# Longer runs of half-array fp32 products, and forget-gate and sparse queries and keys computed transposed, in a two-block transformer kernel

## The chip, the cores and the metric

The kernel runs on one core of one Trainium2 chip. The metric is device time in microseconds (us) of one execution: the median of several runs. The engines named below are PE (TensorE, matrix products, with its weight loads listed apart as PEld), DVE (VectorE), ACT (ScalarE), POOL (GpSimd) and SP (SyncE, which here issues nearly all transfers).

## The reference

Two transformer blocks over 256 tokens of width 1024, all in fp32. Only what the change touches is shown. In the first block one projection of the normalised input gives four attention branches: A (sparse: compressed, selected and windowed keys; 4 heads of 64), B (dilated; 3 groups of 2 heads of 64), C (forgetting; 4 heads of 64) and D (latent; 4 heads of 96).

```python
def nsa_mixer(q, kv_a, ...):                                   # branch A
    k_cmp, v_cmp, k_slc, v_slc, k_win, v_win = split(kv_a, 6)
    kc = gelu((blocks(k_cmp) + cmp_pos) @ phi_k_w1) @ phi_k_w2 # 15 blocks of 32*64 numbers, hidden width 128
    vc = gelu((blocks(v_cmp) + cmp_pos) @ phi_v_w1) @ phi_v_w2
    # softmax(q kc), softmax(q k_slc + bias), softmax(q k_win + bias), each times its values, mixed by gates
def forgetting_mixer(q, k, v, f_logits, f_bias):               # branch C
    cum = cumsum(log_sigmoid(f_logits + f_bias))
    logits = q k / 8 + cum[query] - cum[key]                   # causal softmax, then times v
```

In the second block a retention of 8 heads of 64 computes (q k^T * decay) v without a softmax, and a differential attention of 4 heads forms two causal softmaxes of 64-wide queries and keys each.

## The kernel before

All tensors stay on the chip; the weights stream in from HBM, mostly as panels of 128 x 1024 numbers (512 KB). A panel is loaded by SP into one of 3 `raw` buffers, and `W` (L479) splits it into two parts: `hi`, a copy rounded by ACT, and `lo`, the remainder, by DVE (8 buffers each). The large products (`lin` L597, `mm3` L492) are three single-pass products: hi by hi, hi by lo, lo by hi. `lin` has the input as the stationary operand and gives tokens on partitions ("natural"): 48 products of 512 columns for 512 outputs. `linT` (L624) has 128 weight columns stationary and gives the result transposed, outputs on partitions: 8 products of 512 columns and 8 of 256 for 128 outputs.

The attention products are plain fp32, and each of them shows as two instructions in the trace. Those of heads 64 wide use half of the PE array: in `scores` (L645) the two heads of a pair stand on partitions 0 to 63 and 64 to 127 and are issued in turn (form 64*128 in the trace), and in `values` (L675) the two heads' results go to partitions 0 to 63 and 64 to 127 (form 128*64). `plan.glue()` keeps the four products of such a call together in PE's order. `attend` (L684) is scores, softmax and values of one pair. In branch C the queries and keys are natural (`evac1` L891), get two more columns that carry the cumulated gate, so 66 in all, and 16 PE transposes turn them (L975). Branch A's queries and keys are natural too (`evac2` L962, `evac3` L984) and are turned by 12 transposes (L995). The compressed keys of branch A come from L1065 to L1121: their weights `w1` go through `W` as four panels, the 15 blocks of keys and of values, in hi and lo parts, are a stationary operand of 60 columns, and 16 products with `hi` and 16 with `lo` accumulate. Retention (L1453) has four pairs of heads, each with one run of scores and 6 products of 64 columns with the full array; the differential attention (L1482) has one run of scores for each head.

Every instruction is first recorded. A planner (`Plan`, L17) then simulates the engines, with a cost for each instruction (`_Op`, L347) and the buffers as slots (8 PSUM banks among them), repeats this 120 times with changed priorities, and issues all in the order of the shortest simulated run. So the order on each engine and on SP's queue is fixed by the planner's costs, and each change of a cost may change all of the order.

Of the kernel before, what the change touches and what calls it, by code (L numbers as in the profile page):

```python
# [20 lines left out]
class Plan:  # L21
# [137 lines left out]
    @contextmanager  # L159
    def glue(self):  # L160

        self.gluing = True
        yield
        self.gluing, self.glued = False, None

    def trial(self, prio):
# [29 lines left out]
        while done < len(ops):  # L196
# [15 lines left out]
            for e, hp in heaps.items():  # L212
# [3 lines left out]
                while hp:  # L216
                    pr, n = heapq.heappop(hp)
                    if n in ran:
                        o = None
                        continue  # L220
                    o = ops[n]
                    ok = True
                    for nm in o.own:
                        if nm in place:
                            continue
                        c = self.cls[nm]
                        need = 1 if order[c][ptr[c]] == nm else 1 + (99 if o.dma else self.reserve.get(c, 99))
# [122 lines left out]
class _Op:  # L350
    def __init__(self, plan, n, eng, go, name, outs, ins, k):
# [8 lines left out]
        elif eng == "PE":  # L360
            n_ = size if name == "matmul" else 128
            if name == "transpose":
                self.cost = 108.0
            elif ins[0].dtype == F32R:
# [53 lines left out]
def emit(ctx, tc, nc, T, out, dbg):  # L418
# [226 lines left out]
    def scores(qk, bias, mn, at):  # L645

        ps = [psS([128, 384]) for _ in qk]
        ss = [sb([128, 384], "k2", name="s") for _ in qk]  # L650
        plan.hold = list(ss)
        with plan.glue():
            for tt in (1, 0):
                for p, (q, k) in zip(ps, qk):
                    PE.matmul(p[:, COLS[tt]], q[:, tt * 128:tt * 128 + 128], k[:, :128 * (tt + 1)], start=True, stop=True)
        for tt in (1, 0):
            for u, (p, s) in enumerate(zip(ps, ss)):
                c = at(tt, u)
                V.tensor_tensor_reduce(s[:, COLS[tt]], p[:, COLS[tt]], bias[u][tt], 1.0, 3e38, op0=OP.add, op1=OP.min,
                                       accum_out=mn[:, c:c + 1])  # L660
        return ss
# [13 lines left out]
    def values(po, pts, vs, first, last):  # L675

        blocks = ((0, slice(0, 256), slice(0, 256)), (1, slice(128, 256), slice(256, 384)))
        with plan.glue():
            for n, (j, c, w) in enumerate(blocks if first else blocks[::-1]):
                for u in range(2):  # L680
                    PE.matmul(po[64 * u:64 * u + 64, c], vs[u][j], pts[u][:, w], start=first and n == 0,
                              stop=last and n == 1, skip_group_check=first and last)

    def attend(po, qk, bias, vs, gain=None, first=True, last=True):  # L684

        mn, den, rec = small(4), small(4), small(4)
        ss = scores(qk, bias, mn, lambda tt, u: 2 * tt + u)
        for tt in (1, 0):
            for u in range(2):
                c = slice(2 * tt + u, 2 * tt + u + 1)  # L690
                expo(ss[u], tt, mn[:, c], den[:, c])
        V.reciprocal(rec, den)
        if gain is not None:
            for tt in range(2):
                V.tensor_mul(rec[:, 2 * tt:2 * tt + 2], rec[:, 2 * tt:2 * tt + 2], gain(tt))
        for u in range(2):
            for tt in (1, 0):
                AN.scale(ss[u][:, COLS[tt]], ss[u][:, COLS[tt]], rec[:, 2 * tt + u:2 * tt + u + 1])
        pts = [transP(s) for s in ss]
        values(po, pts, vs, first, last)  # L700
# [17 lines left out]
def mats1(E):  # L718
# [170 lines left out]
    cq, ck, cv = {}, {}, {}  # L889

    def evac1(_, tt, acc):  # L891
        a = acc.rearrange("p (b h d) -> p b h d", b=2, h=4)
        q = sb([128, 4, 66], "k2", name="cq")
        k = sb([128, 4, 66], "k2", name="ck")
        S.mul(q[:, :, :64], a[:, 0], rq8[tt])
        V.tensor_scalar(k[:, :, :64], a[:, 1], rx[tt], None, op0=OP.mult)
        cum = cps[:, tt, :]
        V.tensor_scalar(q[:, :, 64], cum, -1.0, None, op0=OP.mult)
        V.memset(q[:, :, 65], 1.0)
        V.memset(k[:, :, 64], 1.0)  # L900
        V.tensor_copy(k[:, :, 65], cum)
        cq[tt], ck[tt] = q, k

    lin(h, [(two(T["wi1"]), 512)], evac1)
# [43 lines left out]
    def plain(q, k, v, kd, key):  # L948

        oT = heads(key, 2)  # L950
        for p in range(2):
            hs = (2 * p, 2 * p + 1)
            po = psS([128, 256])
            attend(po, [(q[:kd, h], k[:kd, h]) for h in hs], [(cm(0), cm(1))] * 2,
                   [[v[j][:, h, :] for j in range(2)] for h in hs])
            outT(oT, p, po)
# [3 lines left out]
    aqd = {}  # L960

    def evac2(_, tt, acc):  # L962
        v = sb([128, 4, 64], "k1", name="cv")
        V.tensor_scalar(v.rearrange("p h d -> p (h d)"), acc[:, :256], rx[tt], None, op0=OP.mult)
        cv[tt] = v
        q = sb([128, 256], "k1", name="aq")
        S.mul(q, acc[:, 256:], rq8[tt])
        aqd[tt] = q

    lin(h, [(two(T["wi2"]), 512)], evac2)  # L970

    cqT = sb([128, 4, 256], "k4", name="cqT")
    ckT = sb([128, 4, 256], "k4", name="ckT")
    for tt in range(2):
        for src, dst, e in ((cq[tt], cqT, 0), (ck[tt], ckT, 1)):  # L975
            tp = psS([128, 4, 128])
            for i in range(4):
                PE.transpose(tp[:66, i, :], src[:, i, :], ident)
            AN.copy(dst[:66, :, tt * 128:tt * 128 + 128], tp[:66])
    plain(cqT, ckT, cv, 66, "c")  # L980

    akn, av = {}, {}

    def evac3(_, tt, acc):  # L984
        k = sb([128, 4, 2, 64], "k2", name="ak")
        S.mul(k, acc[:, :256].rearrange("p (c d) -> p c d", c=4)[:, :, None, :].to_broadcast([128, 4, 2, 64]), rx[tt])
        v = sb([128, 128], "k1", name="av")
        V.tensor_scalar(v, acc[:, 256:384], rx[tt], None, op0=OP.mult)
        akn[tt], av[tt] = k, v

    lin(h, [(two(T["wi3"]), 384)], evac3)

    aqT = sb([128, 2, 256], "k4", name="aqT")
    akT = sb([128, 4, 256], "k4", name="akT")
    for tt in range(2):  # L995
        tp = psS([128, 2, 128])
        for i in range(2):
            PE.transpose(tp[:, i, :], aqd[tt][:, i * 128:(i + 1) * 128], ident)
        AN.copy(aqT[:, :, tt * 128:tt * 128 + 128], tp)
        tp = psS([128, 4, 128])  # L1000
        for i in range(4):
            PE.transpose(tp[:, i, :], akn[tt][:, i].rearrange("p a d -> p (a d)"), ident)
        AN.copy(akT[:, :, tt * 128:tt * 128 + 128], tp)
# [5 lines left out]
    def evac4(_, tt, acc):  # L1009
        bv[tt] = bvs[:, tt]  # L1010
        S.mul(bv[tt].rearrange("p a b -> p (a b)"), acc, rx[tt])
# [4 lines left out]
    for c in range(6):  # L1016
        acc = linT(h, T["wi5"][c], psA)
        t = sb([128, 256], "k1", name="bqk")
        if c < 3:
            S.mul(t, acc[:, 0], -0.125)  # L1020
            V.scalar_tensor_tensor(t, acc[:, 1], -0.125, t, op0=OP.mult, op1=OP.add)
        else:
            S.copy(t, acc[:, 0])
            V.tensor_add(t, acc[:, 1], t)
        V.tensor_mul((bq if c < 3 else bk)[:, c % 3], t, rT)
# [36 lines left out]

    gate(0, "d")

    posT = sb([128, 16], "sm", name="posT")  # L1065
    G.dma_start(posT, T["posT"])
    w2 = sb([128, 2, 64], "k1", name="w2")
    G.dma_start(w2, T["w2"])
    blk = sb([128, 16, 60], "k8", F32R, name="blk")
    for kv in range(2):  # L1070
        t = sb([128, 16, 15], "k1", name="blkf")
        for par in range(2):
            base = akT[par * 64:(par + 1) * 64, kv, par:par + 1]
            src = bass.AP(tensor=base.tensor, offset=base.offset, ap=[list(base.ap[0]), [2, 16], [16, 15]])
            V.tensor_add(t[par * 64:(par + 1) * 64], src,
                         posT[par * 64:(par + 1) * 64, :, None].to_broadcast([64, 16, 15]))
        hh = blk[:, :, 15 * kv:15 * kv + 15]
        S.copy(hh, t)
        V.tensor_sub(blk[:, :, 30 + 15 * kv:45 + 15 * kv], t, f(hh))
    hp = psS([60, 256])  # L1080
    for c in range(4):
        hi, lo = W(T["w1"][c], 1024)
        for i in range(4):
            k = 4 * c + i
            w = slice(i * 256, (i + 1) * 256)
            if k == 15:
                PE.matmul(hp[:30], blk[:, k, :30], lo[:, w], start=False, stop=False)
            PE.matmul(hp, blk[:, k, :], hi[:, w], start=k == 0, stop=k == 15)
            if k < 15:
# [670 lines left out]
```

## Time and profile before

| what | value |
|---|---|
| time, median of 3 runs | 871.64 us (871.44 to 871.86) |
| time of the profiled execution | 872.01 us |
| span of the profiled execution | 870.2 us, mean granted clock 0.997 |
| PE busy | 858.7 us, 99% |
| DVE busy | 663.0 us, 76% |
| ACT busy | 479.5 us, 55% |
| POOL busy | 45.3 us, 5% |
| chain that ended last | PE 89%, DVE 5%, issue 2% |

The span runs from the first instruction to the last, and the profiled execution's own time lies 1.8 us above it. Busy time is the union of an engine's instructions; matrix products overlap at their ends, so the time that one of them costs PE is read from start to start in the timeline, not from its length.

### The profile page before, as it was taken

The numbers are of one execution on the slowest core, as the hardware profiler recorded it, in microseconds if no ns is written. First come the engines' busy times: TensorE is split into PE (matmuls) and PEld (weight loads), VectorE is DVE, ScalarE is ACT, GpSimd is POOL, SyncE is SP. The second block draws the span as 40 slices with busy tenths as digits, with TensorE's granted clock in tenths as the row PEclk, the third lists the DMA queues.
The fourth block names the chain that finished last, engine by engine and source line by source line (L and its number), as shares of the span: only waits on it lengthen the run. The fifth ranks groups of instructions, "written<-read, shape, count | busy, mean of one in ns | idle before, by whom it ended". The sixth has DMA issues, their size and how long they took to land.

```text
span 870.2 us, 12251 instructions
## 1 busy us (share of the span) xinstructions
PE 858.7 (99%) x4453; PEld 719.8 (83%) x4453; DVE 663.0 (76%) x1201; ACT 479.5 (55%) x810; POOL 45.3 (5%) x58
## 2 busy tenths in 40 slices
PE   8999999999999999999999999999999999999998
PEld 7789877778887888888878887888888888888886
DVE  6986766775778999898988677968775687776663
ACT  5775564764555766655654357645644545544440
POOL 2100000000001000000010111201100000000000
PEclk9999999999999999999999999999999999999999
DMA  7657745466447666666536564454643566666641
GB/s 225 207 191 217 218 148 164 160 198 213 144 148 241 195 212 211 204 195 192 193 122 198 167 194 149 143 169 145 208 131 97 187 200 216 215 182 185 198 141 49
DMA packets 45200, 156.07 MB, mean 179 GB/s; under 512 B 5142, under 2 KB 6984, under 8 KB 45012
## 3 DMA queue, kind: packets, MB, share of 16 engines
q1 hardware_dynamic: 44228, 153.09, 56.1%
q0 software_dynamic: 896, 2.19, 0.8%
q8 instruction: 35, 0.57, 0.3%
q14 instruction: 25, 0.20, 0.1%
q10 hardware_dynamic: 16, 0.00, 0.0%
HBM read 154.21 MB, written 1.06 MB: 178 GB/s over the span
## 4 chain that ended last, share of the span: by engine, by line
PE 89%; DVE 5%; issue 2%; ACT 1%; DMA 1%; POOL 1%; DVEq 0%; POOLq 0%; ACTq 0%
PE bank L102 89%; DVE k L102 2%; DVE lo L102 1%; DVE x L102 1%; POOL sm L102 1%; DMA raw<-in_fdn 1%; DMA raw<-in_fupn 1%; ACT x L102 0%; DVE sm L102 0%; ACT junk L102 0%; ACT k L102 0%; ACT hi L102 0%; ACT k L112 0%; DVEq L1756 0%; ACT sm L102 0%
## 5 line engine op out<-in xcount | busy, mean ns | idle before, releaser
L102 PE MATMUL bank<-hi,x 128*128 128x512 f32 (+3 forms) x1556 | 494.3, 392 | 2.2 <-DVE x L102 1.4
L102 DVE TENSOR_TENSOR lo<-raw,hi 128x1024 fp32r<-128x1024 f32 (+3 forms) x280 | 334.7, 1203 | 79.5 <-ACT hi L102 77.9
L102 ACT CAST hi<-raw 128x1024 fp32r<-128x1024 f32 (+3 forms) x280 | 288.7, 1036 | 140.2 <-PE bank L102 57.9
L102 PEld LDWEIGHTS bank<-hi,x 128*128 128x128 f32 (+1 forms) x1556 | 288.5, 188 | 57.6 <-ACT hi L102 2.5
L102 PE MATMUL bank<-lo,x 128*128 128x512 f32 (+3 forms) x786 | 305.7, 391 | 2.7 <-DVE lo L102 2.2
L102 PEld LDWEIGHTS bank<-lo,x 128*128 128x128 f32 (+1 forms) x786 | 146.6, 187 | 33.0 <-DVE lo L102 4.5
L102 PE MATMUL bank<-x,hi 128*128 128x512 f32 x656 | 167.9, 392 | 0.0
L102 PEld LDWEIGHTS bank<-x,hi 128*128 128x128 f32 x656 | 119.2, 189 | 21.3
L102 PEld LDWEIGHTS bank<-x,lo 128*128 128x128 f32 x656 | 89.7, 190 | 6.5
L102 PE MATMUL bank<-x,lo 128*128 128x256 f32 x656 | 91.8, 282 | 0.0
L112 ACT COPY k<-bank 128x256 f32<-128x256 f32 (+3 forms) x78 | 31.1, 409 | 56.8 <-PE bank L102 52.3
L102 POOL TENSOR_TENSOR sm<-sm,nhalf 128x1 f32<-128x1 f32 (+3 forms) x36 | 35.8, 997 | 492.8 <-DVE sm L102 492.8
L102 PE MATMUL bank<-ident,k 128*128 128x128 f32 (+3 forms) x347 | 53.3, 275 | 1.0 <-DVE k L102 0.7
L102 PEld LDWEIGHTS bank<-ident,k 128*128 128x128 f32 (+3 forms) x347 | 41.5, 138 | 13.8 <-DVE k L102 4.7
L102 DVE TENSOR_TENSOR x<-bank,x 128x512 fp32r<-128x512 f32 (+4 forms) x62 | 36.2, 606 | 20.4 <-PE bank L102 19.4
L102 PE MATMUL bank<-k,k 64*128 64x256 f32 (+12 forms) x364 | 49.9, 327 | 0.7 <-ACT k L112 0.6
L102 PEld LDWEIGHTS bank<-k,k 64*128 64x128 f32 (+4 forms) x364 | 38.7, 176 | 11.5 <-issue 4.9
L102 DVE COPY k<-bank 128x256 f32<-128x256 f32 (+7 forms) x60 | 28.1, 473 | 22.3 <-PE bank L102 22.0
L102 DVE TENSOR_TENSOR k<-k,bank 128x256 f32<-128x256 f32 (+1 forms) x78 | 32.5, 418 | 8.2 <-ACT k L112 7.5
L102 ACT ACTIVATE k<-bank,sm 128x256 f32<-128x256 f32 (+1 forms) x38 | 20.0, 554 | 28.4 <-PE bank L102 17.4
L102 DVE SCALAR_TENSOR_TENSOR k<-k,k,k 128x255 f32<-128x255 f32 x72 | 34.3, 479 | 1.5 <-ACT k L102 0.7
L102 ACT ACTIVATE k<-k,sm 128x128 f32<-128x128 f32 (+1 forms) x60 | 26.6, 446 | 7.5 <-DVE sm L102 7.4
(121 smaller groups left out, 439.4 us busy)
## 6 DMA issues: line engine op xcount, KB each, us to landing
raw<-in_wi SPq DMA_DIRECT2D x42, 512.0 KB, 4.4
raw<-in_up SPq DMA_DIRECT2D x40, 512.0 KB, 4.1
raw<-in_fup SPq DMA_DIRECT2D x36, 512.0 KB, 4.3
raw<-in_wg SPq DMA_DIRECT2D x32, 512.0 KB, 4.3
raw<-in_fdn SPq DMA_DIRECT2D x22, 512.0 KB, 4.5
raw<-in_dn SPq DMA_DIRECT2D x22, 512.0 KB, 4.6
raw<-in_xkv SPq DMA_DIRECT2D x16, 512.0 KB, 4.3
raw<-in_wo SPq DMA_DIRECT2D x8, 512.0 KB, 4.4
```

The source lines that it names most:

```text
L102: op = _Op(self, n, eng, lambda: getattr(target, name)(*map(self.place, a), **{x: self.place(y) for x, y in k.items()}), name, outs, ins, k)
L112: alt = _Op(self, n, e2, lambda: getattr(t2, n2)(*map(self.place, a2), **k2), n2, outs, ins, k2)
```

## The change

Five things change together.

1. `scores`, `values` and `attend` take a list of jobs, and the products of all jobs stand in one glued group. Branches C and D and the differential attention put two pairs (or two heads) in a group, branch A its two kinds of keys, branch B two pairs and one pair for scores and three pairs for values.
2. Retention's scores are grouped by two pairs. Its values use `values` too, which leaves them transposed, so each pair is copied and turned back by two transposes: 8 more transposes and 4 more copies.
3. Queries and keys of C and A come from `linT` (`turned`). C's gate term is no longer in two more columns: a tile of bias, written to DRAM as 8 rows of 128 and read back on all partitions (512 KB), is combined with the mask by 8 DVE instructions. A's two key pairs are also copied to the other half of the partitions by 4 transfers. All of this is issued by SP. The 28 transposes of C and A and the copies after them go.
4. The compressed keys use fp32 weights as they are: no `W`, and 32 products of 128 columns in which 15 stationary columns go in turn to partitions 0, 32, 64 and 96 of the result, in two glued groups.
5. The planner charges half-array and 15-column products less and each glued group 300 ns more, and lets a group take several buffers of a kind at once.

```diff
-    def glue(self):
+    def glue(self, extra=300.0):
         self.gluing = True
         yield
+        self.glued.cost += extra
         self.gluing, self.glued = False, None
...
+            elif plan.gluing and m == 15:
+                self.cost = n_ / 2.4 + 2.0
+            elif plan.gluing and (m == 64 or p == 64):
+                self.cost = n_ * 2 / 2.4 + 2.0
...
-    def scores(qk, bias, mn, at):
+    def scores(jobs):
...
         with plan.glue():
+            for j, pj in zip(jobs, ps):
+                for tt in (1, 0):
+                    for p, (q, k) in zip(pj, j[0]):
+                        PE.matmul(p[:, COLS[tt]], q[:, tt * 128:tt * 128 + 128], k[:, :128 * (tt + 1)], start=True, stop=True)
...
+    def turned(c, ap, dst, q):
+        acc = linT(h, ap, psA)
+        t = sb([128, 256], "k1", name="trn")
+        if q:
+            AN.scale(t, acc[:, 0], -0.125)
+            V.scalar_tensor_tensor(t, acc[:, 1], -0.125, t, op0=OP.mult, op1=OP.add)
+        else:
+            AN.copy(t, acc[:, 0])
+            V.tensor_add(t, acc[:, 1], t)
+        V.tensor_mul(dst, t, rT)
+    cum = sb([128, 8], "sm", name="cum")
...
+    nc.sync.dma_start(scr2, crow)
...
+    nc.sync.dma_start(fox1, bass.AP(tensor=scr2.tensor, offset=scr2.offset, ap=[[0, 128], [1, 1024]]))
...
+    for hh in range(4):
+        V.scalar_tensor_tensor(fox0[:, hh], fox1[:, hh, :128], cum[:, 2 * hh:2 * hh + 1], cm(0), op0=OP.subtract, op1=OP.add)
+        V.scalar_tensor_tensor(fox1[:, hh], fox1[:, hh], cum[:, 2 * hh + 1:2 * hh + 2], cm(1), op0=OP.subtract, op1=OP.add)
+    for c in range(4):
+        turned(c, T["wi1"][c], cqk[:, c], c < 2)
...
-    lin(h, [(two(T["wi3"]), 384)], evac3)
...
+    for c in range(4):
+        turned(c, T["wi3"][c], aqk[:, c], c < 2)
+        if c >= 2:
+            for u in range(2):
+                nc.sync.dma_start(aks[64 * (1 - u):64 * (2 - u), c - 2], aqk[64 * u:64 * u + 64, c])
...
-    for c in range(4):
-        hi, lo = W(T["w1"][c], 1024)
...
+    hp = psS([128, 128])
+    for cc in ((0, 1), (2, 3)):
+        ws = [sb([128, 1024], "g4", name="w1") for c in cc]
...
+        with plan.glue():
+            for c, w in zip(cc, ws):
+                for i in range(4):
+                    for kv in range(2):
+                        r = 32 * (2 * (i % 2) + kv)
+                        PE.matmul(hp[r:r + 15], blk[:, kv, 4 * c + i], w[:, i * 256 + kv * 128:i * 256 + kv * 128 + 128],
+                                  start=c == 0 and i < 2, stop=c == 3 and i > 1)
...
-            PE.matmul(po[0][:, h, :], d[:, :128], rv[0][:, h, :], start=True, stop=True)
-            PE.matmul(po[1][:, h, :], d[:, 128:256], rv[0][:, h, :], start=True, stop=False)
-            PE.matmul(po[1][:, h, :], d[:, 256:], rv[1][:, h, :], start=False, stop=True)
...
+        pT = [psS([128, 256]) for _ in pp]
+        values([(pT[i], ds[i], [[rv[j][:, 2 * p + u, :] for j in range(2)] for u in range(2)], True, True)
+                for i, p in enumerate(pp)])
+        for i, p in enumerate(pp):
+            oT = sb([128, 256], "k1", name="rT")
+            AN.copy(oT, pT[i])
+            for tt in range(2):
+                PE.transpose(po[tt][:, 2 * p:2 * p + 2, :].rearrange("p h d -> p (h d)"), oT[:, tt * 128:tt * 128 + 128], ident)
```

## Rows read from the trace of the kernel before

**Rows 1.** The page: busy us of each engine, its share, instructions

```profile
PE 858.7 (99%) x4453; PEld 719.8 (83%) x4453; DVE 663.0 (76%) x1201; ACT 479.5 (55%) x810; POOL 45.3 (5%) x58
```

**Rows 2.** Waits of PE: total us, times, longest us

```profile
PE bank L102 <- DVE lo L102: 2.2, 3, 1.0
```

**Rows 3.** Timeline of PE, one score run: start us, us, names, form, count

```profile
117.19 0.39 PE L102 MATMUL bank<-hi,x 128*128 128x512 f32 x1
117.51 0.92 PE L102 MATMUL bank<-k,k 64*128 64x256 f32 x8
118.36 0.50 PE L102 MATMUL bank<-hi,x 128*128 128x512 f32 x1
118.70 0.40 PE L102 MATMUL bank<-lo,x 128*128 128x512 f32 x1
```

**Rows 4.** Timeline of PE, a run of three score groups

```profile
534.21 2.23 PE L102 MATMUL bank<-k,k 64*128 64x256 f32 x24
536.38 0.50 PE L102 MATMUL bank<-lo,x 128*128 128x512 f32 x1
```

**Rows 5.** Timeline of PE, a run of two value groups

```profile
147.83 1.52 PE L102 MATMUL bank<-k,k 128*64 128x256 f32 x16
149.28 0.50 PE L102 MATMUL bank<-hi,x 128*128 128x512 f32 x1
```

**Rows 6.** Timeline of PE, transposes and one head pair of branch C

```profile
45.12 1.03 PE L102 MATMUL bank<-ident,k 128*66 128x128 f32 x8
45.91 0.48 PE L102 MATMUL bank<-hi,x 128*128 128x512 f32 x1
46.23 0.40 PE L102 MATMUL bank<-lo,x 128*128 128x512 f32 x1
...
48.29 2.27 PE L102 MATMUL bank<-k,k 66*128 66x256 f32 x16
50.49 0.88 PE L102 MATMUL bank<-ident,k 128*128 128x128 f32 x6
```

**Rows 7.** Timeline of PE, transposed chunks (x,lo) and a natural projection (hi,x)

```profile
84.89 1.11 PE L102 MATMUL bank<-x,lo 128*128 128x256 f32 x8
...
87.68 1.12 PE L102 MATMUL bank<-x,lo 128*128 128x256 f32 x8
...
104.26 0.62 PE L102 MATMUL bank<-hi,x 128*128 128x512 f32 x2
...
111.07 0.61 PE L102 MATMUL bank<-hi,x 128*128 128x512 f32 x2
```

**Rows 8.** Timeline of PE, retention's values with a score run; the kernel's last half-array run

```profile
488.31 3.42 PE L102 MATMUL bank<-k,k 128*128 128x64 f32 x30
491.66 0.50 PE L102 MATMUL bank<-hi,x 128*128 128x512 f32 x1
...
540.77 0.92 PE L102 MATMUL bank<-k,k 64*128 64x256 f32 x8
```

**Rows 9.** Timeline of PE, the compressed keys; in brackets idle us before

```profile
154.44 0.30 PE L102 MATMUL bank<-hi,x 128*60 128x256 f32 x1 [0.82 <-DVE x L102]
...
157.75 0.28 PE L102 MATMUL bank<-hi,x 128*60 128x256 f32 x1
...
161.33 0.63 PE L102 MATMUL bank<-k,k 60*128 60x30 f32 x4
```

**Rows 10.** Two stretches: length, busy us (instructions) of PE, PEld, DVE, ACT, POOL

```profile
20.00:100.00 80.00, 79.66 (x456) 68.20 (x456) 61.86 (x162) 54.02 (x114) 4.31 (x8) 1.00 0.66 207
150.00:165.00 15.00, 13.23 (x83) 10.53 (x82) 14.15 (x38) 7.94 (x20) 0.00 (x0) 1.00 0.50 154
```

**Rows 11.** DVE's groups by form: busy us, mean ns, idle before and releaser

```profile
L102 DVE TENSOR_TENSOR lo<-raw,hi 128x1024 fp32r<-128x1024 f32 x265 | 321.1, 1220 | 77.8 <-ACT hi L102 76.3
L102 DVE TENSOR_TENSOR k<-k,bank 128x256 f32<-128x256 f32 x76 | 31.7, 417 | 8.1 <-ACT k L112 7.5
```

**Rows 12.** Waits of SP's queue: total us, times, longest us

```profile
SPq L102 <- DVE lo L102: 542.5, 217, 13.8
```

More of the change, by code (lines that the diff above doesn't have):

```diff
@@ L226, in trial @@
                         c = self.cls[nm]
-                        need = 1 if order[c][ptr[c]] == nm else 1 + (99 if o.dma else self.reserve.get(c, 99))
+                        k = taken[c] = taken.get(c, 0) + 1
+                        need = k if order[c][ptr[c]] in o.own else k + (99 if o.dma else self.reserve.get(c, 99))
                         if len(free[c]) < need:
@@ L673, in transP, with values @@
         return pT
-    def values(po, pts, vs, first, last):
+    def values(jobs):
         blocks = ((0, slice(0, 256), slice(0, 256)), (1, slice(128, 256), slice(256, 384)))
         with plan.glue():
-            for n, (j, c, w) in enumerate(blocks if first else blocks[::-1]):
-                for u in range(2):
-                    PE.matmul(po[64 * u:64 * u + 64, c], vs[u][j], pts[u][:, w], start=first and n == 0,
-                              stop=last and n == 1, skip_group_check=first and last)
@@ L684, in attend @@
[L684 to L688, printed above, removed]
-            for u in range(2):
[L690 to L700, printed above, removed]
+            for po, pts, vs, first, last in jobs:
+                for n, (j, c, w) in enumerate(blocks if first else blocks[::-1]):
+                    for u in range(2):
+                        PE.matmul(po[64 * u:64 * u + 64, c], vs[u][j], pts[u][:, w], start=first and n == 0,
+                                  stop=last and n == 1, skip_group_check=first and last)
@@ new lines, in attend @@
+    def attend(jobs):
+        mds = [(small(4), small(4)) for _ in jobs]
+        sss = scores([(j[1], j[2], md[0], lambda tt, u: 2 * tt + u) for j, md in zip(jobs, mds)])
+        vals = []
+        for (po, qk, bias, vs, gain, first, last), (mn, den), ss in zip(jobs, mds, sss):
+            rec = small(4)
+            for tt in (1, 0):
+                for u in range(2):
+                    c = slice(2 * tt + u, 2 * tt + u + 1)
+                    expo(ss[u], tt, mn[:, c], den[:, c])
+            V.reciprocal(rec, den)
+            if gain is not None:
+                for tt in range(2):
+                    V.tensor_mul(rec[:, 2 * tt:2 * tt + 2], rec[:, 2 * tt:2 * tt + 2], gain(tt))
+            for u in range(2):
+                for tt in (1, 0):
+                    AN.scale(ss[u][:, COLS[tt]], ss[u][:, COLS[tt]], rec[:, 2 * tt + u:2 * tt + u + 1])
+            vals.append((po, [transP(s) for s in ss], vs, first, last))
+        values(vals)
@@ L950, in plain @@
         oT = heads(key, 2)
+        pos = [psS([128, 256]) for _ in range(2)]
+        attend([(pos[p], [(q[:kd, h], k[:kd, h]) for h in (2 * p, 2 * p + 1)], [(cm(0), cm(1))] * 2,
+                 [[v[j][:, h, :] for j in range(2)] for h in (2 * p, 2 * p + 1)], None, True, True) for p in range(2)])
         for p in range(2):
[L952 to L955, printed above, removed]
@@ new lines, in evac2 @@
+        AN.scale(v, acc[:, 256:384], rx[tt])
+        av[tt] = v
+    lin(h, [(two(T["wi2"]), 384)], evac2)
+    oT = heads("c", 2)
+    pos = [psS([128, 256]) for _ in range(2)]
+    attend([(pos[p], [(cqk[64 * u:64 * u + 64, p], cqk[64 * u:64 * u + 64, 2 + p]) for u in range(2)],
+             [(fox0[:, 2 * p + u], fox1[:, 2 * p + u]) for u in range(2)],
+             [[cv[j][:, 2 * p + u, :] for j in range(2)] for u in range(2)], None, True, True) for p in range(2)])
+    for p in range(2):
+        outT(oT, p, pos[p])
@@ L1005, in mats1 @@
+    aqk = sb([128, 4, 256], "k4", name="aqk")
+    aks = sb([128, 2, 256], "k2", name="aks")
+    for c in range(4):
+        turned(c, T["wi3"][c], aqk[:, c], c < 2)
+        if c >= 2:
+            for u in range(2):
+                nc.sync.dma_start(aks[64 * (1 - u):64 * (2 - u), c - 2], aqk[64 * u:64 * u + 64, c])
     bv = {}
@@ L1016, in mats1 @@
     for c in range(6):
[L1017 to L1025, printed above, removed]
+        turned(c, T["wi5"][c], (bq if c < 3 else bk)[:, c % 3], c < 3)
     mg = [sb([128, 2, 512], "k4", name="merged") for _ in range(2)]
@@ L1080, in mats1 @@
-    hp = psS([60, 256])
-    for c in range(4):
-        hi, lo = W(T["w1"][c], 1024)
[L1083 to L1089, printed above, removed]
-                PE.matmul(hp[:30], blk[:, k, :30], lo[:, w], start=False, stop=False)
-    hn = sb([60, 256], "k1", name="h1n")
@@ L1092, in mats1, with phisrc @@
-    V.tensor_copy(hn, hp)
-    fold = sb([60, 30], "k1", name="fold")
-    V.tensor_add(fold, ident[:60, :30], ident[:60, 30:60])
-    ht = psS([128, 64])
-    for kv in range(2):
-        PE.matmul(ht[:, 32 * kv:32 * kv + 30], hn[:, 128 * kv:128 * kv + 128], fold, start=True, stop=True)
-    h1 = bass.AP(tensor=ht.tensor, offset=ht.offset, ap=[list(ht.ap[0]), [47, 2], [1, 15]])
-    hs = sb([128, 3, 2, 15], "k1", name="gelu")
+    blk = sb([128, 2, 16, 15], "k2", name="blk")
+    def phisrc(kv, par):
+        return (aqk[:, 2] if kv == par else aks[:, 0])[par * 64:(par + 1) * 64, par:par + 1]
@@ new lines, in mats1 @@
+    for kv in range(2):
+        for par in range(2):
+            base = phisrc(kv, par)
+            src = bass.AP(tensor=base.tensor, offset=base.offset, ap=[list(base.ap[0]), [2, 16], [16, 15]])
+            V.tensor_add(blk[par * 64:(par + 1) * 64, kv], src,
+                         posT[par * 64:(par + 1) * 64, :, None].to_broadcast([64, 16, 15]))
+    gate(0, "d")
+    hp = psS([128, 128])
+    for cc in ((0, 1), (2, 3)):
+        ws = [sb([128, 1024], "g4", name="w1") for c in cc]
+        for c, w in zip(cc, ws):
+            plan.bulk = True
+            nc.sync.dma_start(w, T["w1"][c])
+            plan.bulk = False
+        with plan.glue():
+            for c, w in zip(cc, ws):
+                for i in range(4):
+                    for kv in range(2):
+                        r = 32 * (2 * (i % 2) + kv)
+                        PE.matmul(hp[r:r + 15], blk[:, kv, 4 * c + i], w[:, i * 256 + kv * 128:i * 256 + kv * 128 + 128],
+                                  start=c == 0 and i < 2, stop=c == 3 and i > 1)
@@ new lines, in mats1 @@
+    w2, p1, p3 = (sb([128, 256], "k1", name=n) for n in ("p2", "p1", "p3"))
+    w2, w2k = w2[:, :128].rearrange("p (a d) -> p a d", a=2), w2[:, 128:].rearrange("p (a d) -> p a d", a=2)
+    G.dma_start(w2, T["w2"])
+    hn = p1[:, :128]
+    hs = p1[:, 128:218].rearrange("p (i a c) -> p i a c", i=3, a=2)
+    hv = p3[:, :128].rearrange("p (a c) -> p a c", a=4)
+    kc = p3[:, 128:160].rearrange("p (a c) -> p a c", a=2)
+    fold = p1[:, 218:248].rearrange("p (a c) -> p a c", a=2)
+    turn = ident.rearrange("p (a b c) -> p b a c", a=2, b=2)
@@ L1100, in mats1 @@
+    V.tensor_add(fold, turn[:, :, 0, :15], turn[:, :, 1, :15])
+    V.memset(hn, 0.0)
+    for r in (0, 32, 64, 96):
+        AN.copy(hn[r:r + 15], hp[r:r + 15])
+    h1 = psS([128, 2, 15])
+    PE.matmul(h1.rearrange("p a c -> p (a c)"), hn, p1[:, 218:248], start=True, stop=True)
     S.activation(hs[:, 0], h1, AF.Square)
@@ L1186, in mats1 @@
             pts.append(transP(ss[gi][j]))
-        values(po, pts, [[bv[kt][:, 2 * gi + j, :] for kt in range(2)] for j in range(2)], gi == 0, gi == 2)
+        vals.append((po, pts, [[bv[kt][:, 2 * gi + j, :] for kt in range(2)] for j in range(2)], gi == 0, gi == 2))
+    values(vals)
     outT(oT, 0, po)
@@ L1349, in mats2 @@
     rsq, sumsq, split_T, gload, norm_T = g["rsq"], g["sumsq"], g["split_T"], g["gload"], g["norm_T"]
-    scores, expo, transP, recip, COLS = g["scores"], g["expo"], g["transP"], g["recip"], g["COLS"]
+    scores, values, expo, transP, recip, COLS = (g[n] for n in ("scores", "values", "expo", "transP", "recip", "COLS"))
     ident, xs, cm, ropeR, out = g["ident"], g["xs"], g["cm"], g["ropeR"], g["out"]
```

194 lines of the change are left out of this document (76 added, 118 removed).

## The prediction, made before the run

> **What bounds the kernel.** I read the page's busy times first: PE is busy for 99% of the span and DVE for 76% [rows 1]. So a step that takes work from PE should shorten the kernel by that work, one that takes work from DVE or ACT by nothing, unless PE was waiting for it. I then read PE's waits. The largest sum is for DVE's `lo` parts, 2.2 us in three times [rows 2], and it is small. The windows tell where such waits sit: from 150 to 165 us PE is busy for 13.23 of 15 us while DVE is busy for 14.15 [rows 10], which is the stretch of the compressed keys, and one wait of 0.82 us for the stationary operand of these keys stands there [rows 9]. Outside such places PE's work sets the time, and the rest of the reading is of the timeline, from start to start, because a product's own length includes its drain and overlaps the next.
>
> **Prices.** A bulk product of 512 columns costs 0.227 us: 30 of them from 104.26 to 111.07 [rows 7]. A run of half-array products costs more than its products. One score group alone (four products, eight instructions) takes 0.85 us from its start to the next start; but from the bulk product before it to the second one after it there are 1.51 us [rows 3], less two bulk products 1.06. Three groups in one run take 2.17 us [rows 4], so a further group costs 0.66 and entering and leaving a run costs 1.06 - 0.66 = 0.40. Two value groups in a run take 1.45 us [rows 5], 0.13 above 2 x 0.66 where the score run is 0.19 above its group; with that difference a value run's entry and exit cost 0.34. The same products with the full array take 1.31 us a pair (below), twice 0.66, so row halves and column halves already run side by side.
>
> **Part by part, on PE.**
>
> Longer runs. PE's timeline has 18 half-array runs, the first inside the row at 48.29 [rows 6], the last at 540.77 [rows 8], for 15 score and 11 value groups. Retention's and the differential attention's scores already stand as runs of three and one, which become two and two, and branch D's values are one run already: nothing to gain there. Branches A and B have seven score runs and get four: 3 x 0.40 = 1.2 us. Their values are four runs and a fifth that follows a score run directly, and become three: 0.34 and about 0.15. Branch C's two value runs become one: 0.34. Together -2.0 us. This is lost where the planner splits or already joins, and more where it puts glued groups next to each other: either way 0.3 to 0.4 a run.
>
> Branch C's scores. A pair at 66 rows and its values take 2.20 us from 48.29 to 50.49 [rows 6]. The value group is 1.45 - 0.66 = 0.79 of it, and 0.1 is the step into the value run, which is in the price above (before the score run too a bulk product lasts 0.32 instead of 0.227 [rows 3]). That leaves 1.31 for a pair, 2.62 for two. At 64 rows both pairs are one run of two groups, 1.32 + 0.40 = 1.72: -0.9 us.
>
> Transposes. Eight and one bulk product take 1.11 us, so a transpose costs 0.11 [rows 6]. The change takes away 16 of branch C and 12 of A and adds one for the gate: -3.0 us.
>
> Transposed projections. A chunk of 128 outputs takes 2.79 us [rows 7]; a natural one 48 x 0.227 / 4 = 2.72. Eight chunks of 128 move from the one to the other; the natural panel of 384 outputs stays: +0.5 us.
>
> Retention's values. The stretch at 488.31 lasts 3.35 us for 22 instructions of 64 columns and a score run of 0.85 [rows 8], so 0.114 each, 5.45 for all 48 (8 heads, three products, two instructions). After: two runs of two value groups, 2 x (1.32 + 0.34) = 3.3, and 8 transposes, 0.9: -1.25 us.
>
> Compressed keys. From 154.44 to 157.75 there are 28 steps, 0.118 each [rows 9], 3.8 us for 32. The fold of hi and lo was two products (four instructions, 0.63 us with their drain [rows 9]) and becomes one: -0.4. The new products are 64 instructions of 128 columns with 15 stationary columns, in two runs. No row shows four column tiles at once. If each cost what a transpose of 128 columns does and none overlapped, 64 x 0.11 = 7.0; two at a time, which is what the value groups reach [rows 5], 3.5; four at a time 1.8; each with 2 x 0.34 for entering and leaving. I take four at a time, because column halves lose nothing to sharing: a value group costs what a score group does, half of the 1.31 us that as many products of as many columns take with the full array [rows 5, 6]. So 2.4 us against 3.8: -1.4 us. The bounds are +0.4 (two at a time) and +3.9 (none) in place of -1.4.
>
> The Trainium skill speaks against this step: "TensorE: Matmul & The Clock Gate" (Part 3, The mechanism) states that a weight load overlaps running products only when the row group differs, and all column tiles share the rows. This case's value runs, column tiles on all 128 rows, cost a group what the row-tiled score runs do [rows 4, 5], which speaks against the rule here. The same page (Measured speedup vs the span model) gives 2.38 for three column tiles; an estimate by that figure, 7.0 / 2.38 + 0.7 = 3.6 us, would put the sum 1.2 us higher.
>
> Sum on PE: -2.0 - 0.9 - 3.0 + 0.5 - 1.25 - 1.4 - 0.4 = -8.4 us.
>
> **What is not on PE's path.** The four panels of `w1` no longer need `lo`, 4 x 1.22 us of DVE [rows 11], nor `hi` on ACT. That is the stretch with DVE at 14.15 of 15 us, and PE's 15 - 13.23 = 1.8 us of idle time there [rows 10] may go. Against it DVE gets work earlier: eight chunks with two instructions of 256 columns (0.42 us each [rows 11], the third goes to DVE or ACT), 6.7 us, and eight gate-bias instructions, at most 3.4; the copies and scalings that go are worth some 4 us of DVE (an estimate, ten of 0.42). So +6 us in a stretch of 80 us in which DVE is busy for 61.86 [rows 10]; bulk prefetch hides that as long as DVE stays below the span, with 12 us to spare, and if the cover is gone PE waits for part of the 6. The four copies of retention's values (0.42 each) hide behind bulk products, which follow such runs on PE [rows 3, 8]; without that cover PE waits for the last of them. On SP there are two transfers for the gate bias (the 512 KB read one of them) and four swaps of A's keys, which wait for `crow`, for the written rows and for `turned`; behind them in SP's order stand weight panels, and their readers are `hi`, `lo` and then PE. SP mostly waits for DVE's `lo` to free a buffer, 542.5 us in all [rows 12], so panels are not far ahead. I set gain and loss of these at nothing together, between -1.8 and +3.
>
> **How the numbers follow.** The profiled execution took 872.01 us; 872.01 - 8.4 = 863.6. The median of the runs is 0.4 lower than that execution, so 863.2.
>
> **Rivals.** *The column tiles run less than four wide* (chance 0.13): for it, no row shows four, and the rule above; against it, the value groups. Two wide gives 863.2 + 1.8 = 865.0, none 863.2 + 5.3 = 868.5. *DVE becomes the bound in the early projections* (0.13): for it, that DVE is busy there for 77% of the time before the 6 us are added [rows 10]; against it, PE idles there for only 0.34 us of 80 now. Half of the 6 us as waits of PE gives 866. *The runs do not get longer* (0.05), the change not doing what it says: the planner, with other costs, already joined groups before (runs of two and three [rows 4, 5]) and may keep as many runs; without the 2.0 us the time is 865.2. *SP's queue becomes the bound, and the kernel is slower* (0.08): six new transfers wait at SP's head for a producer. If the planner, which does not know real delays, places each 2 us before its data are there beyond what panels in stock cover, that is 12 us, 875. It decides from 10.2 us (8.4 and the 0.2%, 1.8 us, that a measurement of this kernel can tell from no change), 1.7 us for each; against it, `hi` and `lo` have eight buffers each, and a panel is 12 x 0.227 = 2.7 us of PE's work. *A milder form of it or of DVE's bound* eats the gain to within 0.2%, 869.9 to 873.4 (0.06). The forecast itself has 0.55, with its own range 860.5 to 865.5.
>
> Faster by over 0.2%: 0.55 + 0.13 + 0.13 + 0.05 = 0.86; within 0.2%: 0.06; slower: 0.08. The range reaches from 860, the forecast with the whole 1.8 us of idle time gone and some runs joined by chance, to 868.5, the column tiles with no overlap; outside lie the 0.14 of the last two rivals and little of the others.
>
> **What would show it.** Right: some 16 half-array runs besides the compressed keys' two, single pairs of scores for A nowhere; 28 transposes less and 9 more; the compressed keys' two runs near 1.2 us each; chunks of `wi1` and `wi3` at 2.8 us; PE busy about 8 us less with its share still 99%. Wrong: idle time of PE before `lo` or `hi` between 20 and 100 us, or SP waits at the gate bias or the key swaps with late panels behind them; compressed keys' runs of 2 to 4 us; a PE sum that shrinks while the span does not, which would mean that the planner's new order left PE without bulk work in the softmaxes.

## The result, and the profile after

The changed kernel takes 861.55 us (median of 4 runs, 861.05 to 862.52) against 871.66 us of the kernel before: a ratio of 0.9881, 95% interval 0.9869 to 0.9894, so 10.1 us less. The forecast was 863.2 us with a range of 860.0 to 868.5.

The page of the changed kernel, its span and the row that answers to [rows 1]:

```profile
span 859.3 us, 12293 instructions
...
PE 847.7 (99%) x4480; PEld 712.2 (83%) x4480; DVE 662.4 (77%) x1217; ACT 472.2 (55%) x800; POOL 45.3 (5%) x58
```

The span is 10.9 us shorter, and PE is busy for 11.0 us less; its time without work is 11.5 us before and 11.6 after. (These two executions took 872.01 and 861.05 us, so they lie 11.0 us apart, the medians 10.1.) PE executes 27 instructions more. DVE and ACT do almost what they did. So the time came from PE's work, as its share of 99% had said.

The windows, against [rows 10] (columns as there, then granted clock, share of the DMA engines, GB/s):

```profile
20.00:100.00 80.00, 78.67 (x506) 68.90 (x505) 68.92 (x188) 48.60 (x105) 4.86 (x9) 1.00 0.62 205
...
150.00:165.00 15.00, 15.00 (x84) 12.50 (x83) 9.46 (x33) 10.93 (x36) 0.00 (x0) 1.00 0.42 140
```

In the stretch where PE had stood idle for 1.8 us it is now busy throughout. Between 20 and 100 us DVE has 7.1 us more to do (68.92 against 61.86), and PE is idle there for 1.3 us where it was 0.3. So a gain of 1.8 us here and a loss of 1.0 there; the rest of the gain is lost in pieces of up to 0.5 us in other stretches, as PE's time without work is the same over the whole span.

One wait of the new kind, in the timeline of all engines (start us, us, engine, operation, names; rows of PEld and other engines left out):

```profile
30.88 0.16 DVE L102 TENSOR_TENSOR sm<-sm,sm 128x8 f32<-128x8 f32 x1
30.95 1.22 DVE L102 TENSOR_TENSOR lo<-raw,hi 128x1024 fp32r<-128x1024 f32 x1
...
32.09 0.55 DVE L102 TENSOR_TENSOR x<-bank,x 128x384 fp32r<-128x384 f32 x1
...
32.55 0.16 DVE L102 TENSOR_TENSOR sm<-sm,sm 128x8 f32<-128x8 f32 x1
...
32.77 0.38 PE L102 MATMUL bank<-sm,cst 128*128 128x4 f32 x2 [0.66 <-DVE sm L102]
```

The forget gate is a chain of 8-column steps on DVE. Between two of them stand a panel's `lo` (1.22 us) and another remainder (0.55 us), and PE, which goes in order, waits 0.66 us at the cumulated sum.

Half-array runs, in PE's timeline. Branch D's values and branch C's scores joined into one run by the planner (56.64 and 58.09), two score groups in one run (150.19), three value groups in one run (167.79), and retention's scores and values joined like the first (475.49):

```profile
56.64 1.52 PE L102 MATMUL bank<-k,k 128*64 128x256 f32 x16
58.09 1.58 PE L102 MATMUL bank<-k 64*128 64x256 f32 x16
59.59 0.62 PE L102 MATMUL bank<-x,lo 128*128 128x256 f32 x3
```

```profile
149.42 0.39 PE L102 MATMUL bank<-lo,x 128*128 128x512 f32 x1
149.64 0.61 PE L102 MATMUL bank<-hi,x 128*128 128x512 f32 x2
150.19 1.58 PE L102 MATMUL bank<-k,k 64*128 64x256 f32 x16
151.70 0.50 PE L102 MATMUL bank<-lo,x 128*128 128x512 f32 x1
152.03 0.63 PE L102 MATMUL bank<-hi,x 128*128 128x512 f32 x2
...
167.46 0.40 PE L102 MATMUL bank<-lo,x 128*128 128x512 f32 x1
167.79 2.17 PE L102 MATMUL bank<-k,k 128*64 128x256 f32 x24
169.89 0.72 PE L102 MATMUL bank<-hi,x 128*128 128x512 f32 x2
170.45 0.40 PE L102 MATMUL bank<-lo,x 128*128 128x512 f32 x1
...
475.17 0.39 PE L102 MATMUL bank<-lo,x 128*128 128x512 f32 x1
475.49 3.03 PE L102 MATMUL bank<-k,k 64*128 64x256 f32 x32
478.45 0.72 PE L102 MATMUL bank<-hi,x 128*128 128x512 f32 x2
479.01 0.40 PE L102 MATMUL bank<-lo,x 128*128 128x512 f32 x1
```

From 149.64 to 152.03 there are 2.39 us: two bulk products, the run of two groups, and one bulk product after it. Less the three at 0.227 (0.68) the run costs 1.71, as worked out ahead for branch C's scores (1.32 + 0.40 = 1.72). Likewise from 167.46 to 170.45: 2.99 less 0.68 is 2.31 for three value groups, against 3 x 0.66 + 0.34 = 2.32. The joined run, from 475.17 to 479.01, costs 3.84 less 0.68, so 3.16, where two score and two value groups in runs of their own would cost 1.72 + 1.66 = 3.38: joining them saves 0.2 us. There are 14 half-array runs, the first at 56.64, the last at 528.59, where the forecast had 16: the planner joined score and value groups twice.

The compressed keys, in PE's timeline, first of the kernel after, then of the experiment with two column tiles (told below):

```profile
96.47 0.39 PE L102 MATMUL bank<-x,hi 128*128 128x512 f32 x1
96.79 1.07 PE L102 MATMUL bank<-g,k 128*15 128x128 f32 x32
97.79 0.50 PE L102 MATMUL bank<-hi,x 128*128 128x512 f32 x1
98.12 0.39 PE L102 MATMUL bank<-lo,x 128*128 128x512 f32 x1
```

```profile
96.90 0.39 PE L102 MATMUL bank<-x,hi 128*128 128x512 f32 x1
97.22 1.93 PE L102 MATMUL bank<-g,k 128*15 128x128 f32 x32
99.08 0.50 PE L102 MATMUL bank<-hi,x 128*128 128x512 f32 x1
```

The 32 instructions of a run take 1.00 us from start to start (96.79 to 97.79), and 1.86 us when they use two tiles. Four column tiles do share the array. With its neighbours a run costs 1.20 us (96.47 to 98.12, less two bulk products).

### The profile page after: what moved, and what is told of

Same layout as the page of the kernel before. It is cut to its first block, busy times and chain, and to the rows that moved or that the text cites. A ratio compares the mean times of both kernels' runs of the same rounds, so it can differ in the third digit from the quotient of the medians.

```text
span 859.3 us, 12293 instructions
## 1 busy us (share of the span) xinstructions
PE 847.7 (99%) x4480; PEld 712.2 (83%) x4480; DVE 662.4 (77%) x1217; ACT 472.2 (55%) x800; POOL 45.3 (5%) x58
## 4 chain that ended last, share of the span: by engine, by line
PE 93%; DVE 3%; ACT 2%; DMA 1%; issue 1%; POOL 1%; DVEq 0%; ACTq 0%; POOLq 0%; SPq 0%
PE bank L102 93%; DVE x L102 1%; DVE k L102 1%; DVE lo L102 1%; DMA raw<-in_fdn 1%; ACT hi L102 1%; POOL sm L102 1%; ACT junk L102 0%; ACT L102 0%; ACT x L102 0%; DVE sm L102 0%; ACT k L112 0%; ACT k L102 0%; ACT sm L102 0%; ACT x L112 0%
## 5 line engine op out<-in xcount | busy, mean ns | idle before, releaser
L102 PE MATMUL bank<-hi,x 128*128 128x512 f32 (+2 forms) x1476 | 468.2, 392 | 1.8 <-ACT hi L102 1.2
L102 PEld LDWEIGHTS bank<-hi,x 128*128 128x128 f32 x1476 | 274.9, 188 | 55.3 <-ACT hi L102 1.8
L102 PE MATMUL bank<-lo,x 128*128 128x512 f32 (+2 forms) x738 | 289.5, 393 | 1.6 <-DVE lo L102 1.5
L102 PE MATMUL bank<-x,hi 128*128 128x512 f32 x720 | 185.3, 393 | 0.0
L102 PEld LDWEIGHTS bank<-lo,x 128*128 128x128 f32 x738 | 138.8, 188 | 30.2 <-DVE lo L102 3.0
L102 PE MATMUL bank<-ident,k 128*128 128x128 f32 (+2 forms) x327 | 50.2, 274 | 2.1 <-DVE k L102 1.4
L102 PEld LDWEIGHTS bank<-ident,k 128*128 128x128 f32 (+2 forms) x327 | 39.2, 139 | 13.2 <-DVE k L102 4.9
L102 DVE COPY k<-bank 128x256 f32<-128x256 f32 (+5 forms) x56 | 24.1, 436 | 22.3 <-PE bank L102 21.8
L102 PE MATMUL bank<-k,k 128*64 128x128 f32 (+9 forms) x312 | 39.7, 332 | 0.0
L102 PEld LDWEIGHTS bank<-k,k 64*128 64x128 f32 (+3 forms) x312 | 29.3, 168 | 8.3 <-issue 3.1
```

The source lines that it names most:

```text
L102: op = _Op(self, n, eng, lambda: getattr(target, name)(*map(self.place, a), **{x: self.place(y) for x, y in k.items()}), name, outs, ins, k)
```

## The experiments

Each was timed side by side with the kernel before. Times are medians; the ratio is to the kernel before, with its 95% interval. Span and PE's busy time are those of the profiled execution. The kernel before took 871.71 us beside the second seeds, costs_only and short_runs, 871.76 beside natural, the two runs of the keys and ret_full, and 872.55 beside the other four. The changed kernel stood beside none of them, so a difference to its 861.55 us is uncertain by up to some 0.9 us besides the scatter.

| run | us | ratio | span, PE busy |
|---|---|---|---|
| seed2_before | 873.55 | 1.0022 (1.0013 to 1.0032) | 871.8, 860.2 |
| costs_only | 873.3 | 1.0015 (1.0005 to 1.0024) | 871.8, 858.9 |
| seed2_after | 864.86 | 0.9925 (0.991 to 0.994) | 862.4, 851.7 |
| seed3_after | 863.31 | 0.9903 (0.9876 to 0.9931) | 862.9, 852.0 |
| short_runs | 868.12 | 0.9962 (0.9949 to 0.9975) | 865.9, 853.8 |
| natural | 867.03 | 0.9941 (0.9926 to 0.9956) | 865.2, 854.6 |
| keys_split | 865.36 | 0.9926 (0.991 to 0.9943) | 864.3, 853.2 |
| keys_two_wide | 863.4 | 0.9908 (0.9887 to 0.993) | 861.7, 849.8 |
| ret_full | 866.27 | 0.9937 (0.9916 to 0.9958) | 867.0, 855.5 |
| ret_full_again | 864.73 | 0.9913 (0.9898 to 0.9927) | 862.3, 850.0 |
| b_three | 861.08 | 0.9874 (0.9859 to 0.9889) | 859.1, 849.4 |
| rounds400 | 860.44 | 0.9865 (0.9848 to 0.9881) | 858.7, 848.2 |

**Is it the work or the order?** The change moves every instruction, since the planner starts afresh. My theory is that PE's work sets the time and the order moves it by little; the rival is that the new plan happened to come out well. Three runs change the order and leave the products.

```diff
-        pick = random.Random(1)
+        pick = random.Random(2)
```

seed2_before, this edit in the kernel before: 

> The kernel before, with another seed for the planner's search, so another order of the same work. Work theory (PE's work sets the time, the planner's order moves it by little): 871.7 within 1.5. Order theory (the change gained because its plan came out well): moves by 3 us or more.

seed2_after, the same in the changed kernel: 

> The changed kernel with another seed for the planner's search. Work theory: 861.6 within 1.5. Order theory: 865 or more, since a lucky order would be lost.

seed3_after, with 3 in place of 2: 

> The changed kernel with a third seed for the planner's search. If the first seed's order was a lucky one: about 864.9, as the second seed gave. If the second was an unlucky one: 861.6 within 1.

costs_only, in the kernel before:

```diff
         yield
+        self.glued.cost += extra
...
+            elif plan.gluing and (m == 64 or p == 64):
+                self.cost = n_ * 2 / 2.4 + 2.0
```

> The kernel before with the planner's new costs alone (half-array products at half, 300 ns for each glued group, several buffers at once); no product changes. Work theory: 871.7 within 1.5. Order theory: a good part of the 10 us, 867 or less.

The kernel before came out 1.9 us slower with the other seed and 1.6 us slower with the new costs alone; the changed one 3.3 and 1.8 us slower. So the gain is not the planner's: its costs alone give none, and with the second seed on both sides the change still gains 873.55 - 864.86 = 8.7 us. But my theory that order moves it by little is not borne out for the changed kernel: its medians span 3.3 us over three seeds, and the first is the best of them. The second seed's loss is clear: all its runs lie above those of the first (864.20 to 866.39 against 861.05 to 862.52). The third seed's is not: two of its four runs took 861.61 and 861.97 us, like the first seed, and the profiled one (864.66) holds a stretch at half clock that cost it some 1.6 us (last section).

**Longer runs.** short_runs, each pair in a glued group of its own:

```diff
-        with plan.glue():
-            for po, pts, vs, first, last in jobs:
+        for po, pts, vs, first, last in jobs:
+            with plan.glue():
                 for n, (j, c, w) in enumerate(blocks if first else blocks[::-1]):
```

and likewise in `scores` and in retention. 

> The changed kernel with each pair's scores and each pair's values in a glued group of its own again, 32 groups. Work theory: some 22 to 26 half-array runs where the changed kernel has 14, each 0.34 to 0.40 us, so 3 to 4.5 us more, 864.6 to 866. Order theory: anything within 1.5 of 861.6, because the planner joins groups by itself.

It takes 868.12 us, 6.6 more, above what I expected. Its timeline has 25 half-array runs besides the two of the compressed keys, 11 more than the changed kernel: 11 x 0.34 to 0.40 are 3.7 to 4.4 us. The rest, 2 to 3 us, is of the size of the order's spread and is not attributed; against the two other seeds it is 3.3 and 4.8 us slower.

**Queries and keys from stationary weights.** natural puts branches C and A back:

```diff
-    for c in range(4):
-        turned(c, T["wi1"][c], cqk[:, c], c < 2)
+    lin(h, [(two(T["wi1"]), 512)], evac1)
...
-    lin(h, [(two(T["wi2"]), 384)], evac2)
+    lin(h, [(two(T["wi2"]), 512)], evac2)
...
+    plain(cqT, ckT, cv, 66, "c")
...
+    lin(h, [(two(T["wi3"]), 384)], evac3)
```

> The changed kernel with the queries and keys of C and A natural and turned again, C's gate in two more columns (66 rows), no gate-bias tile, no key swaps; all else as changed. Work theory: 28 - 1 transposes at 0.11 (3.0), C's scores with the full array (0.9), less 8 chunks at 0.07 (0.5): 3.4 us more, 865.0. Rival (the bias tile, the swaps and the DVE work cost about what the part saves, through waits between 20 and 100 us): 862 to 863.

867.03 us: 5.5 us more than the changed kernel, 2.2 and 3.7 more than it with the other seeds. The rival, that the bias tile and the swaps eat up the part's gain, falls. The 3.4 us lie inside what the order leaves open. One of their terms can be read apart from it, as branch D's values stand in a run with branch C's scores here too (the first row holds both):

```profile
54.47 4.34 PE L102 MATMUL bank<-k,k 128*64 128x256 f32 x32
58.57 0.48 PE L102 MATMUL bank<-hi,x 128*128 128x512 f32 x1
```

With C's two pairs at 66 rows the run takes 4.10 us from start to start, with 64 rows 2.95 (56.64 to 59.59 above): 1.15 us for branch C's scores, near the 0.9 of the forecast and the 0.2 that joining saves.

**The compressed keys.** keys_split puts the hi and lo parts back (all else as changed):

```diff
+    for c in range(4):
+        hi, lo = W(T["w1"][c], 1024)
...
+            PE.matmul(hp, blk[:, k, :], hi[:, w], start=k == 0, stop=k == 15)
```

> The changed kernel with the compressed keys' products as before: weights split into hi and lo, 60 and 30 stationary columns, fold by two products. PE's work alone: 1.4 + 0.4 = 1.8 us more, 863.4. Relief theory (the four splits on DVE were what PE waited for in that stretch): 1.8 more on top, 865.2, with idle time of PE in the stretch.

keys_two_wide takes two of the four column tiles:

```diff
-                        r = 32 * (2 * (i % 2) + kv)
+                        r = 32 * kv
...
```

> The changed kernel with the compressed keys' products on two column tiles instead of four (all steps of the keys on partitions 0 to 14, of the values on 32 to 46); same number of products. If column tiles share the array as the value groups do: two runs of 32 instructions at 0.11 a pair, 1.9 us each instead of 1.0, and 863.3. If the products are hidden behind something else: 861.6.

keys_two_wide took 863.4 us, 1.85 more, and its two runs 1.86 us each (shown above): what was expected of tiles that share the array, on the term itself and on the time. keys_split took 865.36, 3.8 us more, which by time alone would fit the relief theory. The windows of keys_split speak against it:

```profile
20.00:100.00 80.00, 78.68 (x476) 67.66 (x475) 70.02 (x211) 53.50 (x128) 4.36 (x8) 0.98 0.62 200
100.00:180.00 80.00, 80.00 (x429) 64.71 (x428) 58.22 (x139) 46.96 (x97) 2.15 (x4) 1.00 0.66 209
```

With the four splits back, PE is busy for all 80 us from 100 to 180. The keys' products stand elsewhere in it, from 119 to 127 us (from 97 to 106 in the changed kernel, from 154 to 162 before). So the idle time of [rows 10] does not need the splits to go; the new order has none there, with or without them. What remains above 1.8 us was not separated into its parts; the profiled execution (866.1 us) holds a stretch at half clock that cost it some 1.5 us (last section), and two of the four runs took 864.40 and 864.62.

**Retention.** ret_full puts the values back on the full array, without the copies and the turning back:

```diff
+                PE.matmul(po[0][:, h, :], d[:, :128], rv[0][:, h, :], start=True, stop=True)
+                PE.matmul(po[1][:, h, :], d[:, 128:256], rv[0][:, h, :], start=True, stop=False)
+                PE.matmul(po[1][:, h, :], d[:, 256:], rv[1][:, h, :], start=False, stop=True)
...
-        values([(pT[i], ds[i], [[rv[j][:, 2 * p + u, :] for j in range(2)] for u in range(2)], True, True)
```

> The changed kernel with retention's values as before: six products of 64 columns a pair with the full array, no copies and no turning back; scores still in groups of two pairs. Work theory: 1.25 us more, 862.8. Rival (the added copies and transposes cost a wait at retention's end): 861 or less.

ret_full_again is the same kernel once more. 

> Retention's values with the full array once more, because the first profile of it had a stretch at half clock at 35 and at 540 us. Work theory: PE's work after the start 1.25 us above the changed kernel's, plus up to 2 us that another order can cost: 862.8 to 865. If the first run's 866.3 comes back with no stretch at half clock, the part is worth more than its products.

866.27 and 864.73 us. The profile of the first has stretches at half clock, that of the second has none after the start; by the second, the part is worth 3.2 us against the changed kernel, and 1.4 and -0.1 against it with the third and the second seed. The rival, that the copies and transposes cost a wait, is not borne out by the times; the 1.25 us are inside the spread and not measured more closely than that.

**A better version.** b_three gives branch B's scores one group:

```diff
-    ss = scores([job(0), job(1)]) + scores([job(2)])
+    ss = scores([job(0), job(1), job(2)])
```

> The changed kernel with branch B's three pairs of scores in one glued group (six PSUM banks at once). Work theory: one run less, 0.4 us less, 861.2, if the order stays. Order theory: the group waits for six banks and the order moves the time by up to 3 us either way.

rounds400 lets the planner search longer:

```diff
-    ROUNDS = 120
+    ROUNDS = 400
```

> The changed kernel with 400 rounds of the planner's search instead of 120, the same seed, so the order it keeps is at least as short in its own simulation. If that simulation ranks orders as the chip does: 860.5 or less. If it does not see what differs between orders: anywhere from 861 to 865.

861.08 and 860.44 us. Both are below the kernel before, clear of its noise. Against the changed kernel they are 0.5 and 1.1 us lower, and the intervals of the ratios overlap, so I don't claim it. The two together are the version I would go on from; they were not run together.

## Why the prediction was right

The forecast was 8.4 us of PE work less; PE's busy time fell by 11.0 us and the time by 10.1. The mechanism was right: PE's work went and its time without work stayed. The sizes were not all right, and 1.7 us more went than the sum has. By the steps of the prediction:

- **Price of a run** (0.40 for scores, 0.34 for values): right. The run of two score groups at 150.19 costs 1.71 us with entry and exit, against 1.72, that of three value groups at 167.79 costs 2.31, against 2.32.
- **Number of runs**: mis-sized. 16 were forecast, 14 came, as the planner twice put value and score groups next to each other. The prediction had this as a possibility at 0.3 to 0.4 us a run and did not count it; the joined run at 475.49 saves 0.2, so some 0.4 us together.
- **A misreading without effect**: the value groups behind branch C's scores [rows 6] cannot be C's own, whose softmax had yet to run; they are branch D's. So D's two value runs became one, and C's were one already. The price of a value group is the same, and so is the sum.
- **Branch C's scores, transposes, projections** (3.4 us together): natural gives 5.5, 2.2 and 3.7 against the three orders. The scores alone give 1.15 against 0.9, 0.2 of it from joining; for the transposes and projections it is no sharper than that.
- **Compressed keys** (1.4 and 0.4 us): right. Two runs of 1.20 us are the 2.4 that four tiles at once had given; on two tiles they cost 1.7 us more, against 1.75. The fold takes 0.14 us from start to start (107.77 to 107.91), so the 0.4 less is borne out too. The rule of the Trainium skill weighed there ("TensorE: Matmul & The Clock Gate", Part 3, The mechanism: loads overlap running products only across row groups) does not agree with this trace: 32 weight loads of 0.096 us each, on tiles that share all rows, and their 32 products fit into 1.00 us. The estimate from that page's figure for three tiles, 3.6 us, was too high.
- **Retention** (1.25 us): not contradicted, and not measured apart from the order.
- **Work off PE's path**, set at nothing: 1.8 us gained from 150 to 165 us, 1.0 us lost from 20 to 100 and 0.9 in all other stretches, so nothing together. That they cancel was not worked out, and is luck. DVE's added work was +7.1 us against an estimate of +6, and behind the gate's chain on DVE stands one wait of 0.66 us; the rival of DVE as the bound named the right place, and a third of its price came. That this wait can also be followed by a stretch at half clock (last section) the prediction had not priced.
- **The rival with SP's queue**: nothing of it. PE's waits for `lo` and `hi` are 1.5 and 1.2 us in all; before they were 2.2 [rows 2] and 0.8. The view of SP's waits, against [rows 12]:

```profile
SPq L102 <- DVE lo L102: 531.4, 217, 13.8
```

- **The order** was left out of the sum, and is the largest uncertainty: 1.9 us for the kernel before, 3.3 for the changed one. With the second seed on both sides the gain is 8.7 us, near the 8.4; with the first, 10.1. Of the 1.7 us above the forecast, joined runs are some 0.4. The rest is not attributed; that the first seed suits the changed kernel better is argued from these two pairs, not shown.

Undoing the parts one at a time costs 6.6 + 5.5 + 3.8 + 3.2 = 19.1 us, nearly twice the whole gain. That need not mean that the parts help one another: each undoing also leaves the best order of the three seeds. Against the mean of the other two (864.1 us) the same four cost 4.0 + 2.9 + 1.3 + 0.6 = 8.8 us. This is an argument, not a measurement of the parts, since stretches at half clock raise some of these medians too.

## What to carry to other kernels

Where PE is busy 99% of the time, price each product from start to start, and price the change of array shape by itself: here 0.34 to 0.40 us for each run, more than half of what a head pair's scores cost themselves (0.66). A part that is undone in a kernel whose order is planned anew must be compared with several orders of the same work, not with the best one. Small stationary operands are worth spreading over all column tiles: a run of 32 instructions took 1.00 us in four tiles and 1.86 in two. And a profile's granted clock belongs beside each time: two executions of one kernel differed by 4.7 us here, most of it in stretches at half clock.

## What the runs showed of the hardware

I had not expected the clock to matter after the start. The windows from 32 to 40 us show it (granted clock is the third number from the end): first the kernel after, then keys_split, then seed3_after, then ret_full.

```profile
32.00:40.00 8.00, 7.34 (x41) 5.70 (x41) 7.73 (x27) 3.07 (x7) 0.00 (x0) 1.00 0.49 150
```

```profile
32.00:40.00 8.00, 7.33 (x29) 5.05 (x29) 5.84 (x20) 1.59 (x4) 0.00 (x0) 0.79 0.49 151
```

```profile
32.00:40.00 8.00, 7.32 (x29) 5.38 (x30) 6.26 (x21) 1.97 (x4) 0.00 (x0) 0.79 0.50 150
```

```profile
32.00:40.00 8.00, 7.15 (x24) 4.49 (x24) 5.54 (x17) 1.51 (x4) 0.00 (x0) 0.68 0.48 149
...
536.00:548.00 12.00, 10.27 (x49) 7.83 (x46) 11.32 (x42) 10.74 (x39) 1.20 (x2) 0.86 0.22 62
```

A mean of 0.79 or 0.68 is a part of the stretch at 1.2 GHz and the rest at 2.4. PE was busy for 7.2 to 7.3 of the 8 us in all four and had waited at the gate's sum just before, as in the timeline above; in the kernel after the clock stayed at 2.4 GHz in the profiled execution, in the three others it fell, and 24 to 29 instructions were done there instead of 41. In ret_full it fell again around 540 us, in the softmax with PE busy for 10.27 of 12 us.

What such a fall costs can be read from one kernel profiled twice. ret_full and ret_full_again issue the same instructions on PE in the same order. From the gate's sum to the first transposes of branch D, first ret_full, then ret_full_again:

```profile
33.33 0.38 PE L102 MATMUL bank<-sm,cst 128*128 128x4 f32 x2 [0.67 <-DVE sm L102]
...
42.03 1.04 PE L102 MATMUL bank<-ident,k 128*96 128x128 f32 x8
```

```profile
32.77 0.38 PE L102 MATMUL bank<-sm,cst 128*128 128x4 f32 x2 [0.66 <-DVE sm L102]
...
38.38 1.04 PE L102 MATMUL bank<-ident,k 128*96 128x128 f32 x8
```

The same products take 8.70 us in the one and 5.61 in the other, whose granted clock is 1.00 there: 3.1 of the 4.7 us by which these two executions differ (868.78 and 864.05 us). In keys_split the same products, in the same order, take 7.15 us, so the fall cost some 1.5; in seed3_after its products take 6.72 where the kernel after, in the same order, takes 5.13, so 1.6. The order and the wait are the same with and without the fall, so they alone do not decide it, and what does stays open. The runs of ret_full scatter from 864.46 to 868.78 us, those of ret_full_again from 864.05 to 865.03. That the scatter of all runs comes from such falls was not shown, since only one execution of a run has a profile; the kernel before, whose clock stayed at 2.4 GHz from 32 to 40 us in its profile, scattered too, from 871.44 to 871.86 us beside the changed kernel and from 870.68 to 873.42 beside the second seeds.
